# Joining the scan and decode steps that stand between the projection matmuls of a retention and HGRN2 step

## The chip, the cores and the metric

The kernel runs on one core of a Trainium2 chip. The metric is the device time of one execution in microseconds (us); the time before is the median of three runs. TensorE (PE) multiplies and transposes, VectorE (DVE) and ScalarE (ACT) work elementwise on SBUF and PSUM, GpSimd (POOL) does small operations and issues transfers, SyncE (SP) issues transfers.

## The reference

One layer of a decoder: 2048 prompt tokens of width 1024, and 8 decode tokens with a state each. Two groups of four heads run on the same normalised input, retention (ret) and HGRN2 (hgrn). Both are a recurrence over tokens, computed in chunks:

```
p = rmsnorm(x, g) @ w_in                       # 1024 -> 4096: rq rk rv rg hq hf hi hgate
# per head, per chunk:
A     = (q @ k.T) * decay, lower triangle       # the scores
o     = A @ v + (q * exp(b)) @ S                # S: state, 128x128
S     = exp(b_last) * S + (k * exp(b_last - b)).T @ v
o_cat = rmsnorm_per_head(o) * g * silu(gate)
y     = x + o_cat @ w_out
```

Retention has rotary positions on q and k and one fixed decay per head; HGRN2 has a forget gate for each channel, so its decay inside a chunk differs from channel to channel. The decode tokens do one step of the same recurrence from given states. All is in fp32; the outputs are y for the prompt and for the decode tokens, and the new states of both.

## The kernel before, in words

**Projections.** They carry most of the work, as Strassen-Winograd products: seven products of half size in place of eight. The program makes 24 units u, three per head and half of the prompt (u%3 gives the kind: 0 hgrn forget gate and query, 1 the gates, 2 ret key and query; u//12 the half of the prompt; (u%12)//3 the head), then 8 output units 24 to 31. Ahead of them stands a value stage. A product (L711) is 12 matmuls with 512 columns (four k steps, and three combinations of the high and low parts of the operands), all at L724, emitted in two halves of six. Its operands are w<u><name> (weights) and x0, x1 or wo<name> (the tokens of half 0 or 1, or the output weights), each split into a high part h and a low part l (x_halve: ScalarE copies, VectorE L567 subtracts).

**What sets the order.** All is emitted through a heap of events: `at(position, f)` puts f at a position, `after(d, f)` at d behind the event that calls it, and popping the heap writes the instructions of all engines. Each engine then works strictly in that order. One unit takes 7 slots; a half product is half a slot, six matmuls. So each event that issues TensorE work falls between two half products: what follows calls it an insertion. Events whose positions have no half product between them stand in one insertion.

**The scan steps** of a head come from the table `REC`: s (scores; L971 for ret, whose result is par; L1055 to L1110 for hgrn, pah and plh), k (L887: four transposes of k into the PSUM tile pkh or pkr, copied by ScalarE to ksh or ksr at L893), u (L898: four matmuls into puh or pur, and the four state updates of VectorE at L910/L912 that read them), o (L914: A·v and q·state into poh or por; ScalarE squares at L925, POOL takes the root at L128/L129 half a slot later, ScalarE scales at L933 one slot later, which frees the PSUM tile), t (L941: transposes poth, potr and the gate). Steps 0 and 1 are the two groups of four chunks. h or r at a name's end is the kind.

**The decode steps**: dec_mm (L627, pdp: products with x of the decode tokens, tile mode 128*32), dec_copy (L638), dec_sel (L642, pds), once per unit below 12; then per head d_load, d_state (VectorE, L1313), d_diag, d_mm (L1325, pd, tile mode), d_sel (L1339, pds).

**PSUM** has two rotating tiles for pah, plh, par, pk and pu ("lv"), two for po, pdp, pd and pds ("o"), one for transposes, three for products.

**Other queues.** x1_one, x1_two, x1_sums prepare the second half's tokens, wo_sums the output weights' combinations (VectorE, stores through POOL); w_s1 to w_s4 and w_split the weights' combinations and splits; swap_events loads and splits the next operands shortly before they are needed, as x1 for unit 12 and wo for unit 24.

Of the kernel before, what the change touches and what calls it, by code (L numbers as in the profile page):

```python
# [11 lines left out]
F32 = mybir.dt.float32  # L12
# [7 lines left out]
P = 128  # L20
# [31 lines left out]
def step_kernel(ctx, tc, a, out):  # L52
# [30 lines left out]
    def at(pos, f):  # L83
        count[0] += 1
        heapq.heappush(ev, (pos, count[0], f))
# [81 lines left out]
    def t_done(t):  # L167
        t_free.append(t_tag.pop(id(t))[0])
# [434 lines left out]
    def w_s3(u):  # L603
        w_add(u, "S3", "A11", "S3", ALU.subtract)
# [33 lines left out]
    def dec_copy(u):  # L638
        dec["e"] = t_get([P, 2 * P], f"de{u}")
        act.activation(dec["e"], dec["pt"], AF.Copy)  # L640
# [8 lines left out]
    def prep_events(u):  # L649
        U = 7 * u  # L650
        if 12 <= u < 24 and SPOOL[u % 3]:
            for n, name in zip((-3.4, -2.4, -1.4, -0.4, 0.6, 1.6, 2.6), W_NAMES):
                at(U + n, lambda name=name: w_reload(u, name))
            return
        for n, name in enumerate(("A11", "S3", "A22", "A12")):
            at(U + {0: -7.6, 1: -8.6}.get(u, -5.2) + 0.5 * n, lambda name=name: w_load(u, name))
        if u < 12:
            at(U - 2.05, lambda: dec_mm(u, 0))
            at(U - 0.9, lambda: dec_mm(u, 1))
            at(U - 0.7, lambda: dec_copy(u))  # L660
            at(U + 0.4, lambda: dec_sel(u))
        at(U - 2.4, lambda: w_s1(u))
        at(U - 1.95, lambda: w_s3(u))
        at(U - 1.9, lambda: w_split(u, "A11"))
        at(U - 1.45, lambda: w_s2(u))
        at(U - 1.4, lambda: w_split(u, "S1"))
        at(U - 0.45, lambda: w_s4(u))
        at(U - 0.4, lambda: w_split(u, "S2"))
        at(U + 0.6, lambda: w_split(u, "S4"))
        at(U + 1.4, lambda: w_split(u, "A12"))  # L670
        at(U + 2.4, lambda: w_split(u, "S3"))
        at(U + 3.2, lambda: w_split(u, "A22"))
# [197 lines left out]
    def tail_steps(half, hd, qcol, kT, kscale, decay, eps, name):  # L870
        box = {}

        def load():
            box["v"] = [s_ctx["up"].tile([P, 4, P], F32, tag="v", name=f"v{name}{g}", bufs=2) for g in range(2)]
            ty, h = divmod(hd, NH)
            for g in range(2):
                sp.dma_start(
                    box["v"][g],
                    v_dram[half][ty][4 * g : 4 * g + 4, :, h * P : (h + 1) * P].rearrange("c t d -> t c d"),
                )  # L880
            box["old"] = None
            if half == 1:
                box["old"] = s_ctx["up"].tile([P, P], F32, tag="S", name=f"so{name}", bufs=2)
                sp.dma_start(box["old"], s_dram[hd])
            box["st"] = s_ctx["up"].tile([P, 4, P], F32, tag="st", name=f"st{name}")

        def kt(g):  # L887
            pt = ps_lv.tile([P, 4, P], F32, tag="lv", name=f"pk{name}{g}")
            for j in range(4):
                c = 4 * g + j  # L890
                pe.transpose(pt[:, j], kT[:, c * P : (c + 1) * P], ident)
            box["ks"] = s_ctx["up"].tile([P, 4, P], F32, tag="ks", name=f"ks{name}{g}")
            act.activation(box["ks"], pt, AF.Copy, scale=kscale)  # L893

        def state(c):
            return box["old"] if c == 0 else box["st"][:, (c - 1) % 4]

        def uu(g):  # L898
            pu = ps_lv.tile([P, 4, P], F32, tag="lv", name=f"pu{name}{g}")
            for j in range(4):  # L900
                pe.matmul(pu[:, j], box["ks"][:, j], box["v"][g][:, j], start=True, stop=True)  # L901
            for j in range(4):
                c = 4 * g + j
                if c < CH - 1:
                    dst = box["st"][:, c % 4]
                else:
                    dst = box["new"] = s_ctx["up"].tile([P, P], F32, tag="S", name=f"sn{name}", bufs=2)
                src = state(c)
                if src is None:
                    dve.tensor_copy(dst, pu[:, j])  # L910
                else:
                    dve.scalar_tensor_tensor(dst, src, decay(c), pu[:, j], op0=ALU.mult, op1=ALU.add)  # L912

        def oo(g):  # L914
            po = ps_o.tile([P, 4, P], F32, tag="o", name=f"po{name}{g}")
            for j in range(4):
                c = 4 * g + j
                src = state(c)
                pe.matmul(po[:, j], s_ctx["A"][:, c], box["v"][g][:, j], start=True, stop=src is None)  # L919
                if src is not None:  # L920
                    pe.matmul(po[:, j], qcol(c), src, start=False, stop=True)  # L921
            ms = sm.tile([P, 4], F32, tag="oms", name=f"oms{name}{g}")
            ob = box["ob", g] = s_ctx["up"].tile([P, 4, P], F32, tag="ob", name=f"ob{name}{g}", bufs=N_OB)
            for j in range(4):
                act.activation(ob[:, j], po[:, j], AF.Square, accum_out=ms[:, j : j + 1])  # L925
            rs = sm.tile([P, 4], F32, tag="ors", name=f"ors{name}{g}")

            def root():
                rsqrt_mean(rs, ms, P, eps)

            def scale():
                for j in range(4):
                    act.activation(ob[:, j], po[:, j], AF.Copy, scale=rs[:, j : j + 1])  # L933

            after(0.5, root)
            after(1.0, scale)
            box["gt", g] = s_ctx["up"].tile([P, 512], F32, tag="gt", name=f"gt{name}{g}", bufs=2)
            t0 = half * HALF + g * 512
            after(1.2, lambda: sp.dma_start(box["gt", g], g_dram[hd, :, t0 : t0 + 512]))

        def tr(g):  # L941
            pt = ps_tr.tile([P, 4, P], F32, tag="tr", name=f"pot{name}{g}")
            for j in range(4):
                pe.transpose(pt[:, j], box["ob", g][:, j], ident)
            gt = box["gt", g]
            dve.tensor_tensor(gt, pt.rearrange("p a b -> p (a b)"), gt, op=ALU.mult)  # L946
            t0 = half * HALF + g * 512
            after(0.6, lambda: pool.dma_start(o_dram[hd, :, t0 : t0 + 512], gt))  # L948

        def last():  # L950
            if half == 0:
                pool.dma_start(s_dram[hd], box["new"])
            elif hd < NH:
                sf = s_ctx["up"].tile([P, P], F32, tag="S", name=f"sf{name}", bufs=2)
                dve.tensor_scalar(sf, box["new"], 1.0 / GAMMA[hd], None, op0=ALU.mult)
                after(0.4, lambda: pool.dma_start(out["new_ret_prompt"][0, 0, hd], sf))
            else:
                pool.dma_start(out["new_hgrn_prompt"][0, 0, hd - NH], box["new"])

        return dict(load=load, k0=lambda: kt(0), k1=lambda: kt(1), u0=lambda: uu(0), u1=lambda: uu(1),  # L960
                    o0=lambda: oo(0), o1=lambda: oo(1), t0=lambda: tr(0), t1=lambda: tr(1), last=last)

    def ret_rec(u):
# [19 lines left out]
            half, h, lambda c: qk("q")[:, c * P : (c + 1) * P], qk("k"), gkd[:, h : h + 1], lambda c: G,  # L983
            epsg[:, h : h + 1], name,
        )
        return dict(t, s0=lambda: score(0), s1=lambda: score(1))

    def hgrn_rec(u):
        half, h = u // 12, (u % 12) // 3
# [503 lines left out]
    for u in range(-6, 32):  # L1493
# [5 lines left out]
        for n, sl in enumerate(SLOTS):  # L1499
# [5 lines left out]
            at(U + s + d + 0.01, lambda u=u, n=n: evac(u, n))  # L1505

    REC = {
# [4 lines left out]
    }  # L1512

    def rec_events(u):
# [33 lines left out]
                dict(T1=-3.6, T2=-1.4, B22=0.8, T3=2.8, T4=6.8))  # L1548
    for base, kind in ((77, "x1"), (161, "wo")):
        swap_events(base, kind, dict(B11=0.6, T1=1.8, T2=4.6, B22=5.8, B21=7.0, T3=8.4, T4=12.2),  # L1550
                    dict(B11=3.4, T1=5.0, T2=7.8, B22=9.0, B21=10.4, T3=11.6, T4=14.4))
    at(84 + 2.2, dec_acts)
    at(84 + 2.4, dec_gates)
    at(84 + 3.2, dec_rotate)
    for hd in range(8):
        p0 = 84 + 7.2 + (3.0, 10.2, 16.5, 21.9, 29.0, 35.5, 42.6, 49.5)[hd]
        at(p0 - 2.5, lambda hd=hd: d_load(hd))
        at(p0 + 2.0, lambda hd=hd: d_state(hd, 0))
        at(p0 + 2.4, lambda hd=hd: d_state(hd, 1))
        at(p0 + 1.9, lambda hd=hd: d_diag(hd))  # L1560
        at(p0 + 3.9, lambda hd=hd: d_mm(hd))
        at(p0 + 4.9, lambda hd=hd: d_sel(hd))
    at(150.2, d_sq)
    at(158.0, d_ms)
    at(163.1, d_od)
# [99 lines left out]
```

## Time and profile before

| | us |
|---|---|
| median of 3 runs (1064.7 to 1066.22) | 1065.7 |
| profiled execution | 1067.49 |
| its span | 1065.7 |
| TensorE busy | 1023.8 (96%) |
| VectorE busy | 776.7 (73%) |
| ScalarE busy | 567.5 (53%) |
| GpSimd busy | 262.9 (25%) |
| mean granted TensorE clock | 0.986 |

The profile is one execution. Times on its rows are us from the span's start; a row of the timeline gives start, duration, engine, source line, operation, output<-inputs, tile or shape, and in brackets the idle time of the engine before the row with what ended it. A row with x8 holds eight records of the profile; an fp32 matmul leaves two records, a transpose one. "128*32" is the array tile that a matmul uses, "128*128" the whole array. The table of waits gives for each engine what it waited for: total us, times, longest.

### The profile page before, as it was taken

Reading aid. Unit: us, or ns where it says so; the run is one execution under the profiler, and the core shown is the slowest. Engines: PE = TensorE matmul, PEld = TensorE weight load, DVE = VectorE, ACT = ScalarE, POOL = GpSimd, SP = SyncE. Lnnn points to the kernel's source line nnn. Section 1 sums busy time; section 2 is a strip of 40 time slices with the busy share of each in tenths; the row PEclk is TensorE's granted clock in tenths of the full one; section 3 lists DMA queues with packets and bytes.
Section 4 is the critical chain, followed back from the end, with each engine's and each line's share of the span. In section 5 each row is a group of like instructions: output and inputs, shape, how many; then the busy total and the mean of one; then the engine's idle time right before and its main releaser. Section 6 shows DMA issues by size and latency. Waiting matters only on the chain.

```text
span 1065.7 us, 22525 instructions
## 1 busy us (share of the span) xinstructions
PE 1023.8 (96%) x8688; PEld 842.2 (79%) x8688; DVE 776.7 (73%) x1343; ACT 567.5 (53%) x1315; POOL 262.9 (25%) x403
## 2 busy tenths in 40 slices
PE   9999989999999999999999999989999988999997
PEld 7778867787787787877778788878788867778885
DVE  8676775878669768867796766876756687777775
ACT  7744423746655565654785455447356475433232
POOL 2501384112322333123111122121201501221111
PEclk9999999999999999999999999999999998999999
DMA  9636648838748857865993993892861667536532
GB/s 328 225 133 232 208 164 317 318 124 310 243 154 320 284 182 277 285 206 208 374 318 107 326 320 116 300 331 88 266 230 61 221 233 269 185 109 202 172 119 79
DMA packets 129900, 238.25 MB, mean 224 GB/s; under 512 B 11601, under 2 KB 68049, under 8 KB 127361
## 3 DMA queue, kind: packets, MB, share of 16 engines
q1 hardware_dynamic: 106944, 158.91, 45.3%
q0 software_dynamic: 22704, 77.64, 19.4%
q8 instruction: 68, 1.11, 0.4%
q14 instruction: 40, 0.32, 0.1%
q10 hardware_dynamic: 144, 0.26, 0.1%
HBM read 150.19 MB, written 89.72 MB: 225 GB/s over the span
## 4 chain that ended last, share of the span: by engine, by line
PE 69%; DVE 9%; DMA 7%; issue 6%; POOL 4%; ACT 3%; SPq 0%; POOLq 0%; DVEq 0%; ACTq 0%
PE aO L724 7%; PE aG L724 6%; PE aR L724 6%; PE aH L724 6%; PE pv L365 4%; PE eG L724 4%; PE eR L724 4%; PE aV L724 3%; PE eO L724 3%; PE eH L724 2%; PE bH L724 2%; PE eV L724 2%; PE bO L724 2%; PE plh L1055 1%; PE bG L724 1%
## 5 line engine op out<-in xcount | busy, mean ns | idle before, releaser
L1422 ACT ACTIVATE yj<-xro 128x512 f32<-128x512 f32 x27 | 17.1, 633 | 74.6 <-DVE xro L573 38.4
L1034 ACT ACTIVATE qh<-kh 128x1024 f32<-128x1024 f32 x24 | 25.5, 1062 | 39.7 <-DVE kh L1020 39.7
L1431 DVE SCALAR_TENSOR_TENSOR xro<-xro,yms,fg 128x1024 f32<-128x1024 f32 (+1 forms) x17 | 20.7, 1222 | 31.8 <-POOL yms L129 29.8
L1020 DVE TENSOR_TENSOR kh<-kh,fph 128x512 f32<-128x512 f32 x48 | 32.9, 684 | 8.2 <-PE plh L1055 7.5
L801 ACT ACTIVATE sg<-g 128x512 f32<-128x512 f32 x28 | 17.7, 633 | 38.7 <-DVE g L573 38.4
L236 POOL TENSOR_TENSOR ms<-ms 128x2 f32<-128x2 f32 x8 | 11.6, 1453 | 89.7 <-ACT xn L232 89.7
L933 ACT ACTIVATE obr<-por,orsr 128x128 f32<-128x128 f32 x64 | 18.3, 369 | 27.8 <-POOL orsr L129 27.8
L1023 DVE TENSOR_TENSOR qth<-qth,fph 128x512 f32<-128x512 f32 x48 | 32.8, 684 | 0.0
L948 POOL DMA_DIRECT2D o_dram<-gth x16 | 8.9, 558 | 93.3 <-DVE gth L946 93.3
L128 POOL TENSOR_SCALAR orsh<-omsh 128x4 f32<-128x4 f32 x16 | 3.8, 236 | 107.4 <-ACT obh L925 107.1
L925 ACT ACTIVATE obr<-por 128x128 f32<-128x128 f32 x64 | 16.7, 275 | 24.7 <-PE por L921 24.7
L933 ACT ACTIVATE obh<-poh,orsh 128x128 f32<-128x128 f32 x64 | 18.0, 364 | 21.7 <-POOL orsh L129 21.7
L754 ACT ACTIVATE vo<-aV 128x512 f32<-128x512 f32 x12 | 7.1, 591 | 39.5 <-PE aV L724 30.9
L808 POOL DMA_DIRECT2D g_dram<-g x29 | 15.8, 544 | 44.1 <-DVE g L804 42.6
L804 DVE SCALAR_TENSOR_TENSOR g<-g,pk,sg 128x512 f32<-128x512 f32 x28 | 20.7, 738 | 7.3 <-ACT sg L801 7.2
L921 PE MATMUL poh<-sth,qth 128*128 128x128 f32 x112 | 22.6, 284 | 3.0 <-DVE sth L912 3.0
L912 DVE SCALAR_TENSOR_TENSOR sth<-sth,fph,puh 128x128 f32<-128x128 f32 x48 | 16.6, 345 | 12.1 <-PE puh L901 10.7
L919 PE MATMUL poh<-vh,A 128*128 128x128 f32 x128 | 24.6, 279 | 0.0
L1428 POOL TENSOR_TENSOR yms<-yms 128x1 f32<-128x1 f32 x16 | 3.0, 185 | 86.0 <-ACT yj L1422 68.3
L919 PE MATMUL por<-vr,A 128*128 128x128 f32 x128 | 24.0, 274 | 0.0
L573 DVE TENSOR_TENSOR xro<-aO,xro 128x512 f32<-128x512 f32 x33 | 22.5, 684 | 1.4 <-PE aO L724 1.2
L925 ACT ACTIVATE obh<-poh 128x128 f32<-128x128 f32 x64 | 16.9, 287 | 9.7 <-PE poh L921 9.6
(1759 smaller groups left out, 3796.0 us busy)
## 6 DMA issues: line engine op xcount, KB each, us to landing
xn<-in_x_prompt SPq DMA_DIRECT2D x32, 256.0 KB, 4.4
v_dram<-vo SPq DMA_DIRECT2D x32, 256.0 KB, 2.2
xro<-in_x_prompt SPq DMA_DIRECT2D x16, 512.0 KB, 4.8
out_y_prompt<-xro POOLq DMA_DIRECT2D x15, 512.0 KB, 3.0
g_dram<-g POOLq DMA_DIRECT2D x29, 256.0 KB, 7.0
xr<-in_x_t SPq DMA_DIRECT2D x12, 512.0 KB, 5.3
vh<-v_dram SPq DMA_DIRECT2D x16, 256.0 KB, 8.0
gth<-g_dram SPq DMA_DIRECT2D x16, 256.0 KB, 5.9
```

The costliest lines, as they stand in the source:

```text
L365: pe.matmul(ps, xx, ww, start=(first and n == 0), stop=(last and n == 2))
L573: dve.tensor_tensor(o, x, y, op=ALU.add)
L724: pe.matmul(ps, w[i], x[j], start=(first and k == 0 and m == 0), stop=(k == 3 and m == 2), skip_group_check=True,)
L804: dve.scalar_tensor_tensor(y, y, ng[:, hd : hd + 1], sg, op0=ALU.mult, op1=ALU.mult)
L919: pe.matmul(po[:, j], s_ctx["A"][:, c], box["v"][g][:, j], start=True, stop=src is None)
L921: pe.matmul(po[:, j], qcol(c), src, start=False, stop=True)
L925: act.activation(ob[:, j], po[:, j], AF.Square, accum_out=ms[:, j : j + 1])
L933: act.activation(ob[:, j], po[:, j], AF.Copy, scale=rs[:, j : j + 1])
L1020: dve.tensor_tensor(kv[:, :, 0, :], kv[:, :, 0, :], two[:, :, 1:2].to_broadcast([P, nb, b]), op=ALU.mult)
L1023: dve.tensor_tensor(qv[:, :, 1, :], qv[:, :, 1, :], two[:, :, 0:1].to_broadcast([P, nb, b]), op=ALU.mult)
L1034: act.activation(kept_k, k, AF.Copy)
L1431: dve.scalar_tensor_tensor(xro[c][:, cc], xro[c][:, cc], ms[:, 0:1], fgb["t"][:, cc], op0=ALU.mult, op1=ALU.mult)
```

## The change

Neighbouring steps are put at positions where they share an insertion. The two transposes of k become one step `k` (the second copy goes to a tile of the shared pool), the two updates become one step `u`, both ret scores one step `s`. VectorE's state updates become steps of their own: `st0` right behind u, `st1` behind the first outputs o0. The two dec_mm, dec_sel, w_s3 and the split of A11 move by 0.05 to 0.3 slots. The decode heads have a table of positions of their own, which repeats every 21 slots; their loads stand 5.0 slots ahead of d_mm, their state updates 2.2 and 1.5 slots ahead of it. In swap_events the splits of B11, T1, T2, B22, B21 and T4 move, for x1 and for wo.

```
-            at(U - 2.05, lambda: dec_mm(u, 0))
-            at(U - 0.9, lambda: dec_mm(u, 1))
-            at(U - 0.7, lambda: dec_copy(u))
-            at(U + 0.4, lambda: dec_sel(u))
+            at(U - 1.97, lambda: dec_mm(u, 0))
+            at(U - 0.7, lambda: dec_mm(u, 1))
+            at(U - 0.65, lambda: dec_copy(u))
+            at(U + 0.7, lambda: dec_sel(u))
...
-        at(U - 1.95, lambda: w_s3(u))
-        at(U - 1.9, lambda: w_split(u, "A11"))
+        at(U - 1.9, lambda: w_s3(u))
+        at(U - 1.85, lambda: w_split(u, "A11"))
...
-            box["ks"] = s_ctx["up"].tile([P, 4, P], F32, tag="ks", name=f"ks{name}{g}")
-            act.activation(box["ks"], pt, AF.Copy, scale=kscale)
+            if g == 0:
+                ks = s_ctx["up"].tile([P, 4, P], F32, tag="ks", name=f"ks{name}{g}")
+            else:
+                ks = t_get([P, 4, P], f"ks{name}{g}")
+            box["ks", g] = ks
+            act.activation(ks, pt, AF.Copy, scale=kscale)
...
-            pu = ps_lv.tile([P, 4, P], F32, tag="lv", name=f"pu{name}{g}")
+            pu = box["pu", g] = ps_lv.tile([P, 4, P], F32, tag="lv", name=f"pu{name}{g}")
             for j in range(4):
-                pe.matmul(pu[:, j], box["ks"][:, j], box["v"][g][:, j], start=True, stop=True)
+                pe.matmul(pu[:, j], box["ks", g][:, j], box["v"][g][:, j], start=True, stop=True)
+            if g == 1:
+                t_done(box["ks", g])
+
+        def st(g):
+            pu = box["pu", g]
             for j in range(4):
                 c = 4 * g + j
...
-        return dict(load=load, k0=lambda: kt(0), k1=lambda: kt(1), u0=lambda: uu(0), u1=lambda: uu(1),
+        def both(f):
+            f(0)
+            f(1)
+
+        return dict(load=load, k=lambda: both(kt), u=lambda: both(uu), st0=lambda: st(0), st1=lambda: st(1),
                     o0=lambda: oo(0), o1=lambda: oo(1), t0=lambda: tr(0), t1=lambda: tr(1), last=last)
...
     REC = {
-        0: (("s0", 12.0), ("s1", 14.8), ("s2", 17.6), ("load", 18.0), ("s3", 20.2), ("k0", 21.7), ("u0", 23.0),
-            ("k1", 23.2), ("o0", 23.9), ("u1", 24.3), ("o1", 25.1), ("last", 25.5), ("t0", 27.2), ("t1", 28.6)),
-        2: (("s0", 11.9), ("load", 12.0), ("s1", 12.7), ("k0", 13.3), ("u0", 14.3), ("k1", 14.5), ("o0", 15.5),
-            ("u1", 15.9), ("o1", 17.2), ("last", 17.6), ("t0", 18.8), ("t1", 20.1)),
+        0: (("s0", 12.1), ("s1", 14.8), ("s2", 17.6), ("load", 18.0), ("s3", 20.2), ("k", 21.7), ("u", 22.8),
+            ("st0", 22.81), ("o0", 23.5), ("st1", 23.7), ("o1", 24.7), ("last", 25.2), ("t0", 27.2), ("t1", 28.7)),
+        2: (("s", 12.05), ("load", 12.0), ("k", 13.3), ("u", 14.6), ("st0", 14.61), ("o0", 15.5), ("st1", 15.7),
+            ("o1", 16.8), ("last", 17.6), ("t0", 19.05), ("t1", 21.7)),
     }
...
-                    dict(B11=3.4, T1=5.0, T2=7.8, B22=9.0, B21=10.4, T3=11.6, T4=14.4))
+                    dict(B11=3.0, T1=6.5, T2=8.2, B22=9.3, B21=10.6, T3=11.6, T4=14.2))
...
-        p0 = 84 + 7.2 + (3.0, 10.2, 16.5, 21.9, 29.0, 35.5, 42.6, 49.5)[hd]
-        at(p0 - 2.5, lambda hd=hd: d_load(hd))
-        at(p0 + 2.0, lambda hd=hd: d_state(hd, 0))
-        at(p0 + 2.4, lambda hd=hd: d_state(hd, 1))
-        at(p0 + 1.9, lambda hd=hd: d_diag(hd))
-        at(p0 + 3.9, lambda hd=hd: d_mm(hd))
-        at(p0 + 4.9, lambda hd=hd: d_sel(hd))
+        mm, sel = ((12.15, 14.75), (17.55, 20.15), (27.25, 28.65))[hd % 3]
+        p0 = 84 + 21 * (hd // 3)
+        at(p0 + mm - 5.0, lambda hd=hd: d_load(hd))
+        at(p0 + mm - 2.2, lambda hd=hd: d_diag(hd))
+        at(p0 + mm - 2.2, lambda hd=hd: d_state(hd, 0))
+        at(p0 + mm - 1.5, lambda hd=hd: d_state(hd, 1))
+        at(p0 + mm, lambda hd=hd: d_mm(hd))
+        at(p0 + sel, lambda hd=hd: d_sel(hd))
```

How this moves instructions shows in the order in which they stand on each engine. The numbers behind a name are only the program's tile counter, and the rows of line 724 are the product matmuls. First TensorE in unit 9, where decode products for unit 10 (pdp) and the scores of the ret head of unit 8 (par) stand. Before:

```order
L724 MATMUL eH_4756<-x0B22h,w9S_4742 128x512
L976 MATMUL par_4926<-qr_4460,kr_4364 128x128 x4
L632 MATMUL pdp_4932<-r10A_4775,xz 32x128 x4
L632 MATMUL pdp_4932<-r10S_4811,xz 32x128 x4
L724 MATMUL bH_4941<-x0B21h,w9A_4763 128x512
...
L976 MATMUL par_4987<-qr_4460,kr_4364 128x128 x4
L724 MATMUL aH_4713<-x0T3h,w9S_4813 128x512
```

and after:

```order
L724 MATMUL bH_4924<-x0B21h,w9A_4765 128x512
L632 MATMUL pdp_4951<-r10A_4777,xz 32x128 x4
L632 MATMUL pdp_4951<-r10S_4810,xz 32x128 x4
L989 MATMUL par_4960<-qr_4456,kr_4349 128x128 x4
L989 MATMUL par_4966<-qr_4456,kr_4349 128x128 x4
L724 MATMUL bH_4924<-x0B21h,w9A_4765 128x512
```

The second score has moved ahead into the insertion of the first, which itself stands half a product (six matmuls of bH) later, with pdp ahead of both scores.

Then TensorE in units 11 and 12, at the hgrn head of unit 9: its k, u and first output. Before:

```order
L891 MATMUL pkh_5783<-ident,kh_4962 128x128 x4
L724 MATMUL eH_5795<-x1T1h,w12S_5668 128x512
...
L901 MATMUL puh_5825<-vh_5656,ksh_5788 128x128 x4
L891 MATMUL pkh_5836<-ident,kh_4962 128x128 x4
L724 MATMUL aR_5408<-x0T4h,w11A_5560 128x512
...
L919 MATMUL poh_5871<-vh_5656,A 128x128 x2
L921 MATMUL poh_5871<-sth_5660,qth_5093 128x128
...
L901 MATMUL puh_5906<-vh_5657,ksh_5841 128x128 x4
L724 MATMUL aH_5760<-x1T2h,w12S_5696 128x512
```

and after:

```order
L891 MATMUL pkh_5777<-ident,kh_4946 128x128 x4
L891 MATMUL pkh_5784<-ident,kh_4946 128x128 x4
L724 MATMUL eH_5794<-x1T1h,w12S_5662 128x512
...
L905 MATMUL puh_5820<-vh_5650,ksh_5782 128x128 x4
L905 MATMUL puh_5825<-vh_5651,ksh_5789 128x128 x4
L724 MATMUL aR_5396<-x0T4h,w11A_5556 128x512
...
L928 MATMUL poh_5859<-vh_5650,A 128x128 x2
L930 MATMUL poh_5859<-sth_5654,qth_5093 128x128
```

Both groups' transposes now stand together, and both updates, with the twelve matmuls of eH between the two insertions.

Last, VectorE around the start of the output units, where woT1 is the first output-weight operand that is split (L567, in two halves) and kr, sw, qr belong to the rotation of the last ret head. Before:

```order
L567 TENSOR_TENSOR woT1l<-woT1l,woT1h 128x1024
L585 TENSOR_TENSOR big<-r24A_9448,big 128x512
L172 TENSOR_TENSOR w24A_9614<-r24A_9448,w24A_9614 128x512
L567 TENSOR_TENSOR woT1l<-woT1l,woT1h 128x1024
L573 TENSOR_TENSOR kr_9351<-bR_9601,kr_9351 128x512
...
L573 TENSOR_TENSOR kr_9351<-kr_9351,sw_9610 128x512
L1020 TENSOR_TENSOR kh_8952<-kh_8952,fph_9282 128x8x64
L1023 TENSOR_TENSOR qth_9061<-qth_9061,fph_9282 128x8x64
L573 TENSOR_TENSOR qr_9444<-aR_9335,qr_9444 128x512
```

and after:

```order
L1037 TENSOR_TENSOR kh_8942<-kh_8942,fph_9276 128x8x64
L1040 TENSOR_TENSOR qth_9058<-qth_9058,fph_9276 128x8x64
L567 TENSOR_TENSOR woT1l<-woT1l,woT1h 128x1024
L573 TENSOR_TENSOR qr_9435<-aR_9319,qr_9435 128x512
...
L819 TENSOR_TENSOR kr_9335<-kr_9335,ctab_5951 128x512
L820 TENSOR_TENSOR big<-big,stab_5953 128x512
L573 TENSOR_TENSOR kr_9335<-kr_9335,big 128x512
L567 TENSOR_TENSOR woT1l<-woT1l,woT1h 128x1024
L573 TENSOR_TENSOR xro_9668<-aO_9690,xro_9668 128x512
```

Both halves of the split have moved behind the first rotation of kr and behind the last products of kh, and the second half now stands behind the second rotation of kr as well.

More of the change, by code (lines that the diff above doesn't have):

```diff
@@ L985, in ret_rec, with scores @@
         )
-        return dict(t, s0=lambda: score(0), s1=lambda: score(1))
+        def scores():
+            score(0)
+            score(1)
+        return dict(t, s=scores)
     def hgrn_rec(u):
```

## The prediction

> **What bounds the kernel now.** I read the busy times first, then the chain of work that ended last, then TensorE's row in time, then its waits.
>
> ```profile
> PE 1023.8 (96%) x8688; PEld 842.2 (79%) x8688; DVE 776.7 (73%) x1343; ACT 567.5 (53%) x1315; POOL 262.9 (25%) x403
> PE 69%; DVE 9%; DMA 7%; issue 6%; POOL 4%; ACT 3%; SPq 0%; POOLq 0%; DVEq 0%; ACTq 0%
> ```
>
> TensorE (PE) is busy for 96% of the span and leads the chain; no other engine passes 73%. TensorE issues in the order written, so the time changes only by what an insertion between product matmuls costs and by what TensorE waits for. Both are visible. First an insertion of the scan's output (sixteen records, full array), then two tile-mode ones (128*32), then one where both were already joined. Columns: start, duration, engine, line, operation, output<-inputs, tile.
>
> ```profile
> 482.79 0.39 PE L724 MATMUL aG<-x0T2h,w10S 128*128 128x512 f32 x1
> 483.02 0.38 PE L919 MATMUL por<-vr,A 128*128 128x128 f32 x2
> ...
> 485.04 0.40 PE L724 MATMUL aG<-x0T2l,w10S 128*128 128x512 f32 x1
> ```
>
> ```profile
> 491.27 0.40 PE L724 MATMUL bG<-x0B21h,w10A 128*128 128x512 f32 x1
> ...
> 492.81 0.50 PE L724 MATMUL bG<-x0B21h,w10A 128*128 128x512 f32 x1
> 493.15 0.39 PE L724 MATMUL bG<-x0B21l,w10A 128*128 128x512 f32 x1
> ```
>
> ```profile
> 664.30 0.40 PE L724 MATMUL bG<-x1B21h,w16A 128*128 128x512 f32 x1
> ...
> 666.30 0.50 PE L724 MATMUL bG<-x1B21h,w16A 128*128 128x512 f32 x1
> ```
>
> ```profile
> 688.80 0.39 PE L724 MATMUL bR<-x1B21h,w17A 128*128 128x512 f32 x1
> ...
> 689.69 0.50 PE L724 MATMUL bR<-x1B21h,w17A 128*128 128x512 f32 x1
> ```
>
> One product step is 483.02 − 482.79 = 0.23 us. Between 482.79 and 485.04 stand two products and the insertion: 2.25 − 2 × 0.23 = 1.79 us, or 0.112 us for each of sixteen records. Nothing visible is left for the boundary: a full-array insertion costs its own records, about 0.01 us more at most. In tile mode the step after the insertion is 0.34 (492.81 to 493.15), 0.11 too long, before the entry is counted. Score insertion alone: 492.81 − 491.27 − 0.23 + 0.11 = 1.42. Decode-state insertion alone: 0.89 − 0.23 + 0.11 = 0.77. Both joined (664.30 to 666.30): 2.00 − 0.23 + 0.11 = 1.88. Joining two tile-mode insertions saved 1.42 + 0.77 − 1.88 = 0.31 us.
>
> TensorE's waits (total us, times, longest us):
>
> ```profile
> PE pdp L632 <- ACT obh L933: 5.8, 3, 1.9
> PE plh L1110 <- DVE qth L1023: 3.0, 1, 3.0
> PE poh L921 <- DVE sth L912: 3.0, 1, 3.0
> PE pd L1330 <- ACT obh L933: 2.1, 1, 2.1
> PE pds L645 <- ACT big L640: 1.3, 1, 1.3
> PE pur L901 <- ACT ksr L893: 1.2, 1, 1.2
> PE pd L1330 <- DVE dS L1313: 1.1, 1, 1.1
> PE pds L1341 <- ACT big L1337: 0.7, 1, 0.7
> PE plh L1055 <- DVE qth L1023: 0.6, 2, 0.3
> ```
>
> **What joining saves.** TensorE goes through the same products and the same other matmuls; by the order, insertions fall from 180 to 130. Six more of the joins are tile mode with tile mode, 6 × 0.31 = 1.9 us. In the other 44 a full-array piece meets a full-array or a tile-mode one. Full with full saves at most the 0.01 above; full with tile saves part of a 0.31 (half, 0.16, is the upper bound for all). Most are full with full, so I take 0.05 each, 2.2 us, between 0.4 and 7.0. Together **4.1 us** (2.3 to 8.9).
>
> The Trainium skill ("TensorEngine Tiling (Array Packing)", Key Properties) says that changing the tiling mode drains TensorE, and it says that of mode changes alone. The rows agree, and the rule speaks against this change: most of its joins change no mode. By the rule alone the joins would be worth the 1.9.
>
> **What waits go away.** The largest is pdp, three times (the decode insertions for units 4, 7 and 10; here the last):
>
> ```profile
> 455.26 0.55 POOL L1177 DMA_DIRECT2D x_dram<-x1B  x1 [4.12 <-DVE x1B L1172]
> 456.16 1.03 POOL L129 TENSOR_TENSOR orsh<-orsh,mhalf 128x4 f32<-128x4 f32 x1
> 457.23 1.14 ACT L933 ACTIVATE obh<-poh,orsh 128x128 f32<-128x128 f32 x4 [5.52 <-POOL orsh L129]
> 458.42 0.50 PE L632 MATMUL pdp<-r10A,xz 128*32 128x128 f32 x8 [1.94 <-ACT obh L933]
> ```
>
> The root of the hgrn head's first outputs (POOL, L129) stands in POOL's queue behind the x1 store L1177, which waited 4.12 us for VectorE. ScalarE's scaling waits for the root, and pdp for the PSUM bank that the scaling frees. The change puts o0 at 23.5, so its root at 24.0 is ahead of the store at 24.4 and the scaling at 24.5; pdp also stands six products later. These waits go: 5.8 us. Behind them TensorE runs slowly (columns: window, length, busy us of PE, PEld, DVE, ACT, POOL, granted clock, DMA share, GB/s):
>
> ```profile
> 455.00:458.60 3.60, 1.66 (x19) 1.39 (x21) 2.87 (x5) 1.37 (x7) 2.36 (x4) 1.00 1.07 361
> 458.60:462.40 3.80, 3.80 (x24) 2.80 (x17) 2.27 (x4) 3.73 (x12) 2.81 (x5) 0.55 0.90 334
> 280.50:285.00 4.50, 4.50 (x17) 3.56 (x14) 2.58 (x4) 4.43 (x14) 3.83 (x6) 0.62 0.82 305
> ```
>
> Lost in them against the 0.98 of the whole trace: (0.98 − 0.55) × 3.80 = 1.6 and (0.98 − 0.62) × 4.50 = 1.6; three times, 4.8. So pdp is worth **10.6**.
>
> The other decode waits: pd on ACT 2.1 and on DVE 1.1, both pds 1.3 and 0.7. The tables put pd after the scaling that frees its bank, the state update 1.5 slots or more ahead of pd, and pds 1.4 to 2.6 slots behind it: **5.2**. The ret head's pur wait of 1.2 goes, since u is now 1.3 slots behind the transposes (18 products, 4.1 us, for 12), and plh's 0.6 lies behind pds or potr of the same insertion: **1.8**. Removed in all 10.6 + 5.2 + 1.8 = 17.6. The two waits of 3.0 I treat below.
>
> **What is added.** (1) In hgrn, u now needs both copies of the eight transposes, with 12 products, 2.7 us, between.
>
> ```profile
> 438.40 0.60 PE L891 MATMUL pkh<-ident,kh 128*128 128x128 f32 x4
> 439.67 0.59 ACT L893 ACTIVATE ksh<-pkh 128x512 f32<-128x512 f32 x1
> 615.02 0.60 PE L891 MATMUL pkh<-ident,kh 128*128 128x128 f32 x4
> 618.05 0.60 ACT L893 ACTIVATE ksh<-pkh 128x512 f32<-128x512 f32 x1
> ```
>
> Four transposes are four records, 0.45, eight are 0.90. Counted from the end of eight, the copy would have begun 439.67 − 439.30 = 0.4 us after them at the first, 618.05 − 615.92 = 2.1 at the second. u's first four matmuls need the first copy alone (0.60), and the second four come 0.9 later, so u starts unhindered if the copy begins within 2.7 − 0.6 = 2.1. Five of the eight heads are like the first, three like the second, and from those three the decode copy ahead of it moves. I take 0, between nothing and 3 × 1; it returns as a rival.
>
> (2) VectorE's work on the last states now stands behind the first outputs. In two ret heads the sums over the output weights are then ahead of it:
>
> ```profile
> 477.75 0.68 DVE L576 TENSOR_TENSOR woT<-wo,wo 128x512 f32<-128x512 f32 x1
> 481.96 0.29 DVE L912 SCALAR_TENSOR_TENSOR snr<-str,pur 128x128 f32<-128x128 f32 x1
> ```
>
> From the first sum to the last state is 482.25 − 477.75 = 4.5 us, which had 18 products (4.1) as cover before o1, and has 12 (2.7) after it. o1 reaches the last state after 1.1 us of its own matmuls: wait 4.5 − 2.7 − 1.1 = 0.7, twice, **1.4**. (3) Both ret scores in one insertion need the second rotated half some 8 products earlier:
>
> ```profile
> 452.84 0.69 DVE L573 TENSOR_TENSOR qr<-qr,sw 128x512 f32<-128x512 f32 x1
> ```
>
> It was done at 453.53, 1.9 us before the scores at 455.43 in this head. Where VectorE is later I estimate 0.5 us in three heads, **1.5** (0 to 4). (4) x1's T3 split comes behind the two A operations of the joined scores, each 0.7: **0.7**. (5) Decode loads are issued 2.8 slots (about 11 us) ahead of the state update; the slowest of these transfers landed 10.3 us after issue:
>
> ```profile
> DMA to landing us min/median/max: 4.4/5.8/10.3
> ```
>
> Hidden, by a little; uncovered it would be 1 or 2 us per head. Added: 1.4 + 1.5 + 0.7 = **3.6** (0 to 10).
>
> **The output stage's start.** The second half of woT1's split moves behind six operations of the rotation:
>
> ```profile
> 872.00 0.48 PE L724 MATMUL eO<-woT1h,w24S 128*128 128x512 f32 x1
> 875.12 0.69 DVE L573 TENSOR_TENSOR kr<-kr,big 128x512 f32<-128x512 f32 x1
> ```
>
> The product that reads it starts at 872.00 and needs the second half six steps later, 873.4. The split's first half (1.1 us) is now just ahead of the rotation, the second right behind L573's 875.12. With 1.1 moved in front of L573 and 1.1 + 0.6 taken out earlier, VectorE ends the split near 875.7: a new wait of 2.3 us, with a slow stretch of 1.6. Against it poh's 3.0 for states and what follows it, about 1.0, go, as these states no longer stand behind the split of woT2. I take 0 (−4 to +4). The 3.0 of plh L1110 is a transfer's and stays.
>
> **Sum.** −17.6 − 4.1 + 3.6 + 0 = −18.1 on the profiled execution's 1067.5: 1049.4. That execution is 1.8 above the median of 1065.7, so **1048 us** as a median.
>
> **The rivals.**
> (A) The waits only move: TensorE reaches each place sooner, VectorE, ScalarE and the loads do not, and the next bank or load holds it. For it: TensorE's rows show a wait ending on ACT or DVE in every decode kind. Against it: at 73% and 53% these engines have slack over the span. Only the joins remain: 1065.7 − 4.1 = 1062.
> (B) Every boundary costs what a tile-mode one does: 50 × 0.31 = 15.5 in place of 4.1, 1037. Against it stands the sixteen-record row, which leaves nothing over.
> (C) The slow stretches do not come from the waits ahead of them, and stay: 1048 + 4.8 = 1053. For it: their clock fell only behind the pause (280.50 to 285.00 and 458.60 to 462.40), and a few loaded transfers run there, 0.82 and 0.90 of the DMA. Against it: 455.00 to 458.60 has a fuller DMA, 1.07, at clock 1.00. The Trainium skill ("TensorE: Matmul & The Clock Gate", Part 1) has the clock fall after an idle window of about 3.4 us; the waits here are 1.94, and the trace shows the stretch right behind them all the same.
> (D) Slower: the joined transposes make u wait in all eight hgrn heads, because ScalarE falls further behind there. If the copy begins 1.2 us (two of its 0.60 operations) later than at 618.05, u waits 1.2, and if a slow stretch of 1.6 follows each time, 8 × 2.8 = 22.4 is lost against 18.1 gained: 1070. It decides from 0.7 us later than that row in every head (8 × 2.3 = 18.4); the row at 439.67 is 1.7 earlier.
>
> That the change does not join what it says is excluded by the order.
>
> **Chances and range.** Forecast 0.63, A 0.17, B 0.05, C 0.07, D 0.08. Low end: the joins at 8.9 and nothing added, 1048 − 4.8 − 3.6 = 1040. High end: A with a little of its spread, 1063. Two tenths are left for D, B and the rest of A. A difference under 0.2%, 2.1 us, counts as none. D gives slower 0.08; the part of A above 1063.6 gives no change, 0.06; the rest is faster, 0.86.
>
> **What would show it.** Right: no pdp wait on obh and none of the slow stretches behind it; insertions of the same records at 0.112 us each; a wait of o1 in two ret heads below 1 us; a wait for woT1l near the output stage. Wrong: u waiting for ksh in most hgrn heads (D); pd or pds again behind ACT or a load (A); slow stretches without a wait ahead (C). It fails most likely by new waits of 2 us that I could not see in the order, since each brings 1.6 more.

## The result and the profile after

The changed kernel takes 1047.6 us (median of four runs, 1046.15 to 1053.06) against 1065.8 for the kernel before: a ratio of 0.984, 95% interval 0.980 to 0.988. A second comparison on another chip gave 1048.5 against 1068.1, ratio 0.983 (0.978 to 0.988). The forecast was 1048 in a range of 1040 to 1063. The chips differ by some us, so experiments below are read by their ratio to the kernel before that ran beside them; 0.001 is 1.07 us. The changed kernel stands at 0.984.

The profiled execution took 1046.15 us, its span 1044.4. Its busy line, and then TensorE's waits of which the rest speaks:

```profile
PE 1015.5 (97%) x8688; PEld 841.1 (81%) x8688; DVE 775.2 (74%) x1343; ACT 564.3 (54%) x1315; POOL 262.3 (25%) x403
```

```profile
PE plh L1127 <- DVE qth L1040: 4.6, 1, 4.6
PE bO L724 <- DVE woB21l L567: 2.1, 1, 2.1
PE eO L724 <- DVE woT1l L567: 2.1, 1, 2.1
PE plh L1072 <- issue: 2.0, 1, 2.0
PE bH L724 <- ACT x1B21h L566: 1.7, 1, 1.7
PE bH L724 <- DVE x1B21l L567: 0.8, 1, 0.8
PE pur L905 <- ACT ksr L897: 0.5, 1, 0.5
PE poh L930 <- DVE sth L921: 0.2, 1, 0.2
```

Every wait of pdp, pd and pds is gone, and pur's fell from 1.2 to 0.5. Among the waits left, four are new, all on splits of the operands that are swapped in at the change of halves (x1B21, twice) and at the output stage (woT1, woB21). poh's 3.0 became 0.2, and the wait behind the transfer of r24A grew from 3.0 to 4.6.

Where the last pdp wait had been, the clock is now full. The columns are again window, length, busy us of PE, PEld, DVE, ACT and POOL, granted clock, DMA share, GB/s:

```profile
448.00:456.00 8.00, 8.00 (x62) 6.74 (x61) 5.94 (x10) 5.68 (x12) 3.56 (x5) 1.00 1.07 371
```

It was 0.55 in the stretch of the kernel before, with the DMA no busier there than here (0.90 against 1.07).

An insertion that now joins transposes, the hgrn score and the decode state (potr, pah, pd):

```profile
566.22 0.39 PE L724 MATMUL bG<-x1B21h,w13A 128*128 128x512 f32 x1
...
568.65 0.50 PE L724 MATMUL bG<-x1B21h,w13A 128*128 128x512 f32 x1
568.98 0.39 PE L724 MATMUL bG<-x1B21l,w13A 128*128 128x512 f32 x1
```

From 566.22 to 568.98 less two products it costs 2.76 − 0.46 = 2.30. Apart, four transposes cost 0.45, and by the prediction's rows the score 1.42 and the decode state 0.77: 2.64. The two joins save 0.34, of which 0.31 was forecast for the one of tile mode with tile mode and 0.05 for the other.

### The profile page after: what moved, and what is told of

Its sections match the earlier page's. It is cut to its first block, busy times and chain, and to the rows that moved or that the text cites. A ratio compares the mean times of both kernels' runs of the same rounds, so it can differ in the third digit from the quotient of the medians.

```text
span 1044.4 us, 22543 instructions
## 1 busy us (share of the span) xinstructions
PE 1015.5 (97%) x8688; PEld 841.1 (81%) x8688; DVE 775.2 (74%) x1343; ACT 564.3 (54%) x1315; POOL 262.3 (25%) x403
## 5 line engine op out<-in xcount | busy, mean ns | idle before, releaser
L801 ACT ACTIVATE sg<-g 128x512 f32<-128x512 f32 x21 | 13.3, 632 | 39.4 <-DVE g L573 34.8
L942 ACT ACTIVATE obr<-por,orsr 128x128 f32<-128x128 f32 x64 | 18.3, 370 | 18.8 <-POOL orsr L129 18.6
L930 PE MATMUL por<-str,qr 128*128 128x128 f32 x112 | 21.7, 276 | 0.0
```

## The experiments

### Only the root ahead of the store (from the kernel before)

```
-        at(p0 + 3.4, lambda k=k: x1_two(k))
+        at(p0 + 3.45, lambda k=k: x1_two(k))
```

> The kernel before, with x1_two alone moved from 3.4 to 3.45, so that the root of the hgrn head's first outputs stands ahead of the x1 store in POOL's queue; nothing is joined. Forecast's theory: the three pdp waits (5.8 us) go and the slow stretches behind them (3 x 1.6 = 4.8) go with them: 1065.8 - 10.6 = 1055. Rival C (the slow stretches have another cause): only the 5.8 go, 1060, and three windows with a clock near 0.6 stay. Rival A (waits only move): another wait takes their place within the unit, 1064 to 1066.

Measured: 1058.8, ratio 0.991 (0.988 to 0.994), 9.7 us less with 6.5 to 12.9 as the interval. The 10.6 lies inside, the 5.8 of rival C outside, and the 0 to 2 of rival A far outside. The waits of pd and of unit 1's pds stand nearly as before, pdp has no row any more. In this run the three pdp start at 277.15, 362.79 and 449.35, and the windows behind them run at full clock:

```profile
PE pd L1330 <- ACT obh L933: 2.3, 1, 2.3
PE pds L645 <- ACT big L640: 1.3, 1, 1.3
```

```profile
277.00:282.00 5.00, 5.00 (x41) 4.08 (x41) 4.93 (x9) 4.75 (x10) 3.99 (x7) 1.00 1.04 376
362.50:367.50 5.00, 5.00 (x42) 4.13 (x41) 4.93 (x9) 4.63 (x10) 4.00 (x7) 1.00 1.06 356
449.00:454.00 5.00, 5.00 (x42) 4.13 (x42) 4.93 (x9) 4.57 (x10) 3.99 (x7) 1.00 1.07 366
```

So three root operations behind three stores in GpSimd's queue cost about 10 us, and the slow stretches followed from the waits. This one moved number brings more than half of the whole change's 18.

### The scan table alone (from the kernel before)

```
-        0: (("s0", 12.0), ... ("k0", 21.7), ("u0", 23.0), ("k1", 23.2), ("o0", 23.9), ("u1", 24.3), ...
+        0: (("s0", 12.1), ... ("k", 21.7), ("u", 22.8), ("st0", 22.81), ("o0", 23.5), ("st1", 23.7), ...
```

and the same for ret, with the joined steps; decode positions and swap_events stay as before.

> The kernel before with the scan table and its steps alone changed (scores, k and u joined, state updates behind the first outputs, o0 earlier); decode positions and swaps as before. 21 insertions fewer, nearly all full array with full array. Forecast's theory: the pdp waits with their stretches go (10.6), pur's 1.2, joins 21 x 0.05 = 1.0, against 1.4 + 1.5 added: 1065.8 - 9.9 = 1056. Rival B (every boundary costs 0.31): 21 x 0.31 = 6.5 in place of 1.0, 1050. Rival A: joins alone, 1065. Rival D (u waits for its copies in the hgrn heads): 1069 or more.

Measured: 1059.9, ratio 0.993 (0.991 to 0.995), 7.2 us less (5.2 to 9.2). The 9.9 of the forecast lies a little outside, and 1069 is far off. No u waits for ksh in any hgrn head (puh has no row), so rival D is out. What was missed are new waits that come from the old decode positions against the new scan:

```profile
PE pds L645 <- ACT de L640: 3.0, 3, 1.0
PE poh L930 <- DVE sth L921: 2.6, 3, 2.1
PE pkh L891 <- DVE kh L1037: 2.2, 2, 1.5
```

The three pds waits, 1.0 each in units below 12, did not exist before. The pd waits of 2.1 and 1.1 are gone here, though the decode heads stand at their old positions.

### The old decode heads (from the changed kernel)

```
+        p0 = 84 + 7.2 + (3.0, 10.2, 16.5, 21.9, 29.0, 35.5, 42.6, 49.5)[hd]
+        at(p0 - 2.5, lambda hd=hd: d_load(hd))
...
```

> The changed kernel with the old positions of the decode heads (load, state, diag, mm, sel); 13 insertions more, six of them tile mode apart from tile mode. Forecast's theory: the waits of pd on ACT 2.1 and on DVE 1.1 and of pds 0.7 come back (3.9), and the joins lost cost 6 x 0.31 + 7 x 0.05 = 2.2: 1047.6 + 6.1 = 1054. Rival A (the heads' waits only moved): 1047 to 1050, joins alone. Rival B (0.31 each): 13 x 0.31 + 3.9 = 7.9, 1055.5, told apart only by the insertions' own rows.

Measured: 1055.5, ratio 0.989 (0.986 to 0.992), 5.5 us more than 0.984. The two intervals just overlap, but the fastest of these four runs (1054.8) is above the slowest of eight runs of the changed kernel (1053.1). The size is near what was expected, the reason is not: no pd wait came back.

```profile
PE pkh L891 <- DVE kh L1037: 1.1, 1, 1.1
PE pds L1358 <- ACT do L1354: 0.3, 1, 0.3
```

Instead of 3.9 the rows have 1.1 and 0.3. 13 insertions more, six of them tile mode apart from tile mode, cost 2.2 by the prediction's prices. The rest lies in rows that differ between executions of one kernel (below), so its place is not shown.

### The old unit positions (from the changed kernel)

```
-            at(U - 1.97, lambda: dec_mm(u, 0))
...
+            at(U - 2.05, lambda: dec_mm(u, 0))
...
```

> The changed kernel with the old positions of dec_mm, dec_copy, dec_sel, w_s3 and the split of A11; 16 insertions more. The run with the scan table alone had waits of pds on ACT de of 3 x 1.0 and on ACT big of 1.3, all of units below 12, which these positions should bring back here: 4.3. With 16 x 0.05 = 0.8 for the joins: 1047.6 + 5.1 = 1053. Rival B: 16 x 0.31 + 4.3 = 9.3, 1057. If the positions are worth nothing but joins: 1048.

Measured: 1056.1, ratio 0.990 (0.987 to 0.993), 6 us more; the fastest run, 1053.8, is again above all eight of the changed kernel. The time alone does not tell the forecast's 5.1 from rival B's 9.3. The expected waits are there to the digit:

```profile
PE pds L645 <- ACT de L640: 3.0, 3, 1.0
PE pds L645 <- ACT big L640: 1.3, 1, 1.3
```

So these positions do two things: they take away unit 1's 1.3 that the kernel before had, and they avoid the 3.0 that the new scan table would bring by itself.

### u apart again (from the changed kernel)

```
-        return dict(load=load, k=lambda: both(kt), u=lambda: both(uu), ...
+        return dict(load=load, k=lambda: both(kt), u0=lambda: uu(0), u1=lambda: uu(1), ...
```

with u1 at 23.05 and 15.05.

> The changed kernel with u in two insertions again (u1 half a slot behind u0), in all 16 heads: 16 full-array boundaries more, same records. What counts is the rows: by the forecast's theory an insertion of four updates costs 8 x 0.112 = 0.90 and two of them 0.01 to 0.02 more than one of eight (1.80), 0.2 in all. By rival B each costs 0.31 more, 5.0 in all.

One execution, 1049.3. The joined u of the changed kernel, and then one of the two here:

```profile
260.34 0.39 PE L724 MATMUL eH<-x0T1h,w3S 128*128 128x512 f32 x1
260.57 1.95 PE L905 MATMUL puh<-vh,ksh 128*128 128x128 f32 x16
...
262.58 0.40 PE L724 MATMUL aR<-x0T4l,w2A 128*128 128x512 f32 x1
```

```profile
261.91 0.39 PE L724 MATMUL eH<-x0T1h,w3S 128*128 128x512 f32 x1
262.14 1.05 PE L905 MATMUL puh<-vh,ksh 128*128 128x128 f32 x8
...
263.26 0.40 PE L724 MATMUL aR<-x0T4l,w2A 128*128 128x512 f32 x1
```

Joined: 2.24 − 0.46 = 1.78. Apart: 1.35 − 0.46 = 0.89, twice 1.78. A boundary of full-array matmuls costs nothing that these rows can show; rival B's 0.31 is excluded for this kind.

### The old splits of the swap (from the changed kernel)

```
-                    dict(B11=3.0, T1=6.5, T2=8.2, B22=9.3, B21=10.6, T3=11.6, T4=14.2))
+                    dict(B11=3.4, T1=5.0, T2=7.8, B22=9.0, B21=10.4, T3=11.6, T4=14.4))
```

> The changed kernel with the old table of splits in swap_events (x1 and wo). In the changed kernel's profile the new table has waits of 2.1 (woT1l), 2.1 (woB21l) and 1.7 + 0.8 (x1B21) with a slow stretch of about 1.3 behind the last: 8.0. The old table had 0.6 (pkh) and 3.0 (poh) with about 1.0 of slow clock: 4.6. If these add up: 1047.6 - 8.0 + 4.6 = 1044. If the new positions fit the joined steps better than the old ones (waits move to the products of the old splits): 1047 to 1052.

Measured: 1047.1, ratio 0.981 (0.977 to 0.984). By ratio that is 3 to 4 us below the changed kernel, as by the first reading (1044 against 1047.6), but the two intervals overlap: no difference is shown. The waits changed places:

```profile
PE poh L930 <- DVE sth L921: 2.3, 2, 2.1
PE bH L724 <- DVE x1B21l L567: 1.7, 1, 1.7
PE bO L724 <- DVE woB21l L567: 0.6, 1, 0.6
```

### Three splits moved ahead (from the changed kernel)

The edit, by its numbers alone:

```
-  B21=10.6 (x1)      T1=6.5, B21=10.6 (wo)
+  B21=9.8 (x1)       T1=6.0, B21=10.0 (wo)
```

> The changed kernel with three of the splits moved ahead, the rest of its table kept: x1's B21 from 10.6 to 9.8, wo's T1 from 6.5 to 6.0 and B21 from 10.6 to 10.0, so that they stand ahead of the rotation on VectorE and of the scaling and squares on ScalarE. If the three waits are only a matter of the queue's order: 1047.6 - 8.0 = 1040, and no wait on woT1l, woB21l or x1B21 is left. Rival A (VectorE has no time there, the wait goes to whatever is pushed back): 1045 to 1048, with waits on kh, sth or qr instead.

Measured: 1048.7, ratio 0.983 (0.979 to 0.987): nothing gained. The waits on the three splits are gone, and others of the same size stand in their place, among them:

```profile
PE par L989 <- DVE qr L573: 2.2, 1, 2.2
PE poh L930 <- DVE sth L921: 2.1, 1, 2.1
PE aO L724 <- DVE woT3l L567: 1.5, 1, 1.5
PE aO L724 <- ACT woT3h L566: 1.4, 1, 1.4
```

Rival A, rejected in the scan stage, holds here. One thing that is different in these stages is VectorE's load. In the changed kernel it is 49.02 of 60 and 44.59 of 50 us, against 74% over the span:

```profile
500.00:560.00 60.00, 56.56 (x341) 48.22 (x342) 49.02 (x89) 43.91 (x100) 7.07 (x11) 0.94 0.76 276
846.00:896.00 50.00, 45.35 (x242) 35.01 (x241) 44.59 (x68) 33.30 (x72) 5.25 (x10) 0.96 0.65 224
```

### VectorE's load made smaller (from the changed kernel)

```
+        w = slice(0, GW if now[0] < 50 else 32)
-        dve.tensor_tensor(l[:, kk], ...
+        dve.tensor_tensor(l[:, kk, w], ...
```

> The changed kernel with VectorE's part of the splits of x1 and wo (L567) made on 32 of 512 columns; this leaves out most of the low parts of these operands. 28 operations of 1.1 us become short, some 28 us of VectorE's 95 us in the two swap stages. If VectorE's load is what sets the waits there: woT1l, woB21l, woT3l and x1B21l go, 1047.6 - 2.1 - 2.3 - 0.8 - 0.7 = 1042, with ScalarE's 1.7 at x1B21h and the transfer's 4.6 kept; 1040 if the stretches go too. If it is only the order of the queue, no different from the splits moved ahead: 1047 to 1049.

Measured: 1041.1, ratio 0.976 (0.970 to 0.981), 7.4 us below the changed kernel's 1048.5 beside it, about what was expected. The intervals of the two ratios overlap a little, but on this chip the slowest run here (1041.4) is below the fastest of the changed kernel (1046.1). The same windows, and the waits on the splits that are left:

```profile
500.00:560.00 60.00, 55.63 (x341) 46.83 (x342) 36.86 (x88) 44.56 (x101) 6.58 (x11) 0.97 0.79 277
846.00:896.00 50.00, 48.40 (x269) 38.72 (x269) 39.31 (x78) 34.22 (x73) 5.68 (x11) 0.98 0.66 228
```

```profile
PE eO L725 <- DVE woT1l L568: 1.1, 1, 1.1
PE bH L725 <- ACT x1B21h L566: 0.9, 1, 0.9
PE bO L725 <- DVE woB21l L568: 0.5, 1, 0.5
```

With 12 us less for VectorE in the first window its wait there vanishes, and with 5 us less in the second 4.2 of waits become 1.6, without any split moved. So less work on VectorE ahead of the product helps where another place in the queue did not. How far the load of the whole stage matters stays open, because the edit also shortens the very operations that TensorE waits for: the two halves of woT1's own split took 1.22 us each before and 0.22 here, which is the whole 1.9 us by which that split ends earlier (855.14 in place of 857.03).

### The loads of unit 24 earlier, alone and with two splits moved

```
-            at(U + {0: -7.6, 1: -8.6}.get(u, -5.2) + 0.5 * n, lambda name=name: w_load(u, name))
+            at(U + {0: -7.6, 1: -8.6, 24: -6.2}.get(u, -5.2) + 0.5 * n, lambda name=name: w_load(u, name))
```

The first change alone, then with wo's splits too, by their numbers alone:

```
-  T1=6.5, B21=10.6 (wo)
+  T1=6.0, B21=10.0 (wo)
```

> The changed kernel with the four loads of unit 24's operands (r24 from o_dram) one slot earlier. In the changed kernel's profile VectorE waits 5.07 us for r24A (landing 10.7 to 11.0 us after issue) and TensorE 4.6 behind it (plh on qth), with a slow stretch of 1.25. If the transfer only starts too late: 1047.6 - 4.6 - 1.25 = 1042, or up to 2 less where woT1l's wait falls too, since VectorE then starts the output stage earlier. If the wait moves (VectorE busy 44.6 of 50 us there and the queue's other loads pushed back): 1045 to 1048.

> The changed kernel with unit 24's loads a slot earlier, and with wo's T1 split at 6.0 and B21 at 10.0 (x1 left alone). The loads alone took the wait of 4.6 away, but left woT1l 3.0 and woB21l 2.1; the splits alone left poh 2.1 and woT3 2.9 with a stretch. If VectorE is short of time there only because it waited 5.07 us for the transfer, both together leave none of these: 1047.6 - 4.6 - 1.25 - 2.1 - 2.3 = 1037. If VectorE is the bound there anyway (44.6 of 50 us busy), the waits come back at woT3 or poh with 2 to 4 us: 1042 to 1045.

Measured: 1045.8, ratio 0.980 (0.977 to 0.983), and 1045.2, ratio 0.980 (0.975 to 0.984). The wait of 4.6 went in both. In the first woT1l took some of it (2.1 before), in the second poh did:

```profile
PE eO L724 <- DVE woT1l L567: 3.0, 1, 3.0
```

```profile
PE poh L930 <- DVE sth L921: 2.8, 1, 2.8
```

By ratio the first lies between the two readings expected for it, and the second within the upper one (1042 to 1045). Both ratios are about 4 us below the changed kernel's and the lowest of the kernels that leave nothing out, though the old splits come within 1 us of them; the intervals overlap with the changed kernel's. A gain of 4 is likely, not shown.

### Part of the load given to GpSimd (from the last kernel)

```
+        eng = pool if now[0] > 50 and b in ("T2", "T3") else dve
-        dve.tensor_tensor(l[:, kk], ...
+        eng.tensor_tensor(l[:, kk], ...
```

> The kernel with early loads and wo's T1 and B21 moved, and GpSimd instead of VectorE for the subtraction in the splits of T2 and T3 of x1 and wo (8 operations of 128x1024). The thin splits showed that VectorE's load sets the waits in the two swap stages. If GpSimd does them in time: poh 2.8 with its stretch of 1.6, woT3l 1.2 and puh 0.9 go, 1045.2 - 6 = 1039 to 1041. If GpSimd is slow at this shape (no run here shows it) or holds the root behind it: new waits on woT2l or woT3l and on the scaling, 1044 to 1050.

Measured: 1049.4, ratio 0.984 (0.982 to 0.986): some 4 us above the kernel it starts from, though the intervals touch. The waits expected to go grew: poh from 2.8 to 4.2, woT3l from 1.2 to 2.4, now on GpSimd. GpSimd's two operations, and VectorE in the same time:

```profile
857.57 5.39 POOL L568 TENSOR_TENSOR woT2l<-woT2l,woT2h 128x1024 fp32r<-128x1024 f32 x2 [19.46 <-ACT woT2h L566]
```

```profile
857.25 0.68 DVE L172 TENSOR_TENSOR w24S<-r24S,w24S 128x512 fp32r<-128x512 f32 x1
857.85 2.90 DVE L820 TENSOR_TENSOR qr<-qr,ctab 128x512 f32<-128x512 f32 x1
860.67 2.83 DVE L821 TENSOR_TENSOR sw<-sw,stab 128x512 f32<-128x512 f32 x1
```

A GpSimd operation took 2.7 us where VectorE needs 1.2, and VectorE's operations beside them took 2.90 and 2.83 in place of 0.68: each ended about 0.5 us after one of GpSimd's two. VectorE lost 2 × 2.2 = 4.4 us to be relieved of 2 × 1.2.

### The changed kernel again

> The changed kernel again, beside the two others on the same chip, as their base: 1047 to 1049. Its waits on woT1l, woB21l and x1B21 should stand in a second profile with the same 2.1, 2.1 and 1.7 + 0.8; the waits that the profile puts down to issue inside plh are expected to differ.

Measured: 1048.5; this profiled execution took 1052.7, 6.5 more than the first. The swap waits are there again (woT1l 2.8 this time, woB21l 2.1, x1B21 1.7 and 0.8). woT1l's wait now has a slow stretch behind it, which the first execution did not have (1.00 from 857 to 862):

```profile
863.00:868.00 5.00, 5.00 (x24) 4.66 (x23) 4.96 (x9) 2.71 (x4) 0.00 (x0) 0.66 0.90 346
```

And inside plh there are more waits for nothing that the profile shows, 5.1 in place of 2.0:

```profile
PE plh L1072 <- issue: 5.1, 2, 2.9
```

```profile
244.00:252.00 8.00, 7.21 (x38) 5.44 (x39) 4.14 (x8) 3.15 (x5) 0.00 (x0) 0.79 0.68 259
505.00:512.00 7.00, 5.88 (x16) 4.66 (x17) 2.95 (x6) 1.58 (x2) 0.76 (x2) 0.52 1.00 371
```

The clocks behind them are 0.79 and 0.52. In the first execution the clock was 1.00 in the window from 244, and 0.76 behind its one wait inside plh, at 501.02:

```profile
500.00:507.00 7.00, 5.98 (x21) 4.76 (x22) 4.65 (x9) 2.07 (x4) 1.08 (x2) 0.76 1.04 392
```

Two stretches elsewhere were longer in the first execution, so over the whole span, summed over windows of 1 us, the slow clock cost at most 11.9 us here against 10.2. TensorE's idle time is 32.4 us against 28.9. These two make 5.2 of the 6.5 us; where the rest went is not shown. So two profiles of one kernel can lie 6 us apart: one profile alone does not decide about 3 us.

## Why the prediction was right

**The bound and pdp.** The step that carried most, 10.6, is shown: its cause by the one moved number (9.7, between 6.5 and 12.9), the 4.8 for slow stretches by the three windows at clock 1.00 in that run. Rival C is out for these three.

**The other decode waits (5.2).** All four rows are gone, so the sum was right, but the step gave the credit to the wrong edits in part. It put pd's 3.2 down to the heads' new positions. With the old heads these waits stay away, and with the scan table alone they are gone: the scan table removes them, most likely by its earlier outputs. The heads' table is worth about 5.5 all the same, by joins (2.2) and by 1.4 of waits that the rows show; what the remaining 2 is stays open. Unit 1's pds was right. That the scan table alone makes three new waits of 1.0, which the unit positions then avoid, was not seen; the parts do not add up as single changes.

**pur, plh (1.8).** pur kept 0.5, plh's 0.6 went: 1.3.

**Joins (4.1).** The checked pieces fit: full array with full array nothing, a join with two tile-mode pieces 0.34. Rival B is out for the full-array kind. The Trainium skill ("TensorEngine Tiling (Array Packing)", Key Properties) says that changes of the tiling mode drain TensorE, and says it of mode changes alone; here the trace agrees: 0.00 for u against 0.31 for the tile-mode pair.

**u behind both copies (0).** Right: no row of u on ksh in the changed kernel. Rival D did not come.

**What is added (3.6).** The sum was too high in its places: no wait of o1 on the last states in the ret heads, none of par worth a row, none of x1T3. Where 0.7 was put for x1's T3, the change of halves has 1.7 and 0.8 at x1's B21, with a slow stretch behind, which the prediction did not look at.

**The output stage's start (0).** woT1l was forecast at 2.3 and measured at 2.1, without the slow stretch of 1.6 behind it; in the second execution it was 2.8 with one, so the 2.3 is close in part by chance. poh fell from 3.0 to 0.2 as said. Missed were woB21l's 2.1 and the growth of plh's wait from 3.0 to 4.6. Not counted either were two waits of the kernel before that have no row any more:

```profile
PE pkh L891 <- DVE kh L1020: 1.8, 2, 1.2
PE pyd L1381 <- DVE A L977: 1.1, 1, 1.1
```

**The sum.** In the rows: −10.6 (pdp) − 5.2 − 1.3 − 4.1 − 2.8 (poh) − 2.9 (pkh, pyd), and + 2.5 (x1B21) + 4.2 (woT1l, woB21l) + 1.6 (plh) = −18.6, against −18.1 forecast and −18.2 between the medians. That the fit is so close is luck. Two errors of some 5 us cancelled: 5.7 of waits went that were set against others at 0 (poh) or not counted (pkh, pyd), and 8.3 of new ones came in the output stage and at x1's B21 in place of the 3.6. All but 1.2 of pkh's 1.8 lie in the two stages where VectorE is most loaded: there waits are exchanged, and rival A, which was given the whole kernel, holds for these 110 us.

The rows also belong to the two profiled executions, which lie 21.3 us apart and not 18.2. Between these TensorE's idle time falls from 41.9 to 28.9, by 13.0, and the loss to the slow clock, summed over windows of 1 us up to TensorE's last work, from at most 13.7 to 10.2. That is 3.5 in all, although pdp's three stretches are gone (4.8 by the forecast), because the profile after has stretches of its own, behind x1B21 among others. The 4.8 that are left hold the joins, put at 4.1 (2.3 to 8.9); no run measures all joins together.

## What to carry to other kernels

Look first at what stands ahead of a small operation in an in-order queue: a root operation behind a store that waits cost 10 us here, half of it in the clock behind the wait, and one number cured it. Joining insertions pays where the tile mode changes (0.3 us each here) and not between full-array matmuls. Before moving work about to remove a wait, read the busy share of the engine it waits for in that window. In 20 us around each pdp wait of the kernel before, ScalarE, for which pdp waited, was busy for 62% and VectorE for 71%, and moving helped; in stages where VectorE was busy for 82 to 89%, moved splits only brought the wait out elsewhere with the same size, and less work helped. Nothing between these shares was tried.

## What the runs showed of the hardware

**VectorE and GpSimd in each other's way.** Two of VectorE's products of two operands took 2.90 and 2.83 us beside a GpSimd subtraction; the median of these lines in the same run is 0.68. The Trainium skill ("SBUF — State Buffer", Who interferes with whom) says that an operation of VectorE with two SBUF inputs contends with one of GpSimd that reads SBUF, and that the ports they share are locked by one of them at a time; the trace agrees with that.

**A wait and the clock behind it.** The same wait of 1.3 us, at unit 1's pds near 206.5, was followed by a slow stretch in the run with the old unit positions and by none in the kernel before (nor with the root ahead of the store, nor with the scan table alone):

```profile
206.00:212.00 6.00, 5.28 (x18) 4.29 (x19) 4.29 (x6) 5.26 (x10) 0.00 (x0) 0.72 0.30 94
```

```profile
206.00:212.00 6.00, 5.47 (x26) 4.61 (x27) 4.44 (x6) 5.61 (x12) 0.00 (x0) 1.00 0.26 85
```

The length of the wait alone does not decide it. The three pdp waits of 1.94 each had a stretch behind them. woT1l's had none after 2.1 us and one after 2.8; woB21l's 2.1 had none in two executions of the changed kernel and one with the old unit positions; plh's 3.0 on qth had one in the kernel before, and the same wait of 2.9 had none with the root ahead of the store. Each stretch, summed over windows of 1 us, lost 1.7 us or twice that: about 3.4 or 6.8 us at a clock of 0.50. So a stretch can follow a wait well below 3.4 us, but need not, and the 1.6 that the prediction adds to each new wait is a price that only some waits pay. The Trainium skill ("TensorE: Matmul & The Clock Gate", Part 1) has the clock fall after an idle window of about 3.4 us, which is longer than any of these waits; it also calls the window free-running, and a dependence on where in a window a wait falls would fit these rows. No run tested that.
